# Up projections of a convolutional SwiGLU block, token-major, with their results turned by VectorE and GpSimd

## The chip, the cores and the metric

The kernel runs on one core of one Trainium2 chip. The metric is device time in microseconds (us); lower is better. A core has engines with a queue each: TensorE (PE; its weight loads are listed apart as PEld), VectorE (DVE), ScalarE (ACT), GpSimd (POOL) and SyncE (SP), which only starts DMAs. An engine takes the instructions of its queue in order, and waits at an instruction until what it needs has been signalled. Matmuls write to PSUM; everything else here lies in SBUF, 128 partitions wide, or in DRAM.

## The reference: what is computed

A trunk of two decoder layers on 256 tokens of width 2048, float32. Layer 0 mixes tokens by gated linear attention, layer 1 by attention over one shared key/value block; each is followed by the same channel mixer, which is what the change touches:

```python
def conv_ffn(x, norm_w, w_up, conv_w, conv_b, w_down):
    S = x.shape[1]
    h = rms_norm(x, norm_w) @ w_up                      # (256, 2048) @ (2048, 11264)
    hp = jnp.pad(h, ((0, 0), (CONV_WIDTH - 1, 0), (0, 0)))
    acc = conv_b
    for j in range(CONV_WIDTH):                         # 3 taps along the tokens
        acc = acc + conv_w[j] * hp[:, j:j + S]
    a, u = jnp.split(acc, 2, axis=-1)                   # 5632 gates, 5632 values
    return (jax.nn.silu(a) * u) @ w_down                # (256, 5632) @ (5632, 2048)
```

The norm factor of a token, 1/sqrt(mean of squares + eps), can be applied after the product, since it is one number per token.

## The kernel before

**Split products.** Every float32 operand is split into a high part of TensorE's rounded format and the rest. For weights ScalarE casts the high part (`whi`, line 143) and VectorE subtracts it (`wlo`, line 145), 1024 columns of a 128-partition tile at a time; such a 128x1024 piece is a *half*, and taking the next half is a *step* (`step`, line 343), the unit in which all delayed work is counted: `after(n, job)` runs a job n steps later. The input's parts lie side by side, 256 tokens high then 256 tokens low (`xw`). A product is high x high + low x high + high x low.

**Weight stream.** SP loads the weights in pieces of 1 MB (`wraw`, three buffers), in the order of `plan`, up to four pieces ahead; the splitting runs two halves ahead of TensorE, three where the plan says "deep" (`prefetch`, line 129), which it does for the up projections.

**The up projection** (`ffn`, line 693). A loop of 44 column groups per layer; group j holds 128 gate columns and the 128 value columns that belong to them. `gemm` (line 352) makes the group feature-major: the weights are the stationary operand (128x128), the input's tokens move past them, so that the result has features on partitions and tokens along the row. For each half, 8 products move 512 columns (both input parts against the weight's high part, line 359) and 8 move 256 (the input's high part against the weight's low part, line 361). ScalarE copies one part of the result out of PSUM (line 387), VectorE adds the other (line 388) and multiplies by the token norm (line 703). The convolution runs along the row, with one constant per partition for each tap: ScalarE makes the last tap with the bias (line 707), VectorE adds the two others (lines 709 and 711). ScalarE applies silu (line 713), VectorE multiplies gate and value (line 714), and the result is split into the `hid` tile (lines 399 and 400), one tile for two groups.

**The other form.** `gemm_tok` (line 365) makes 512 columns at a time token-major: the input is stationary, 512 weight columns move, and the result has tokens on partitions. Each half takes 12 products of 512 columns. Values, queries, keys and shared values use it; their results need tokens on partitions or are turned by TensorE.

**Beside the up projections.** The down projection (`down`, line 725) uses a scheme that saves products in blocks of four for some hidden tiles (marked in `ORDERS`). It needs sums of weights, which `make_ahead` (line 323) prepares while earlier stages run: every nine steps SP loads 1 MB of down weights into one of two `ahead` buffers, VectorE makes four sums (lines 328 and 329), and GpSimd's queue starts the store to DRAM (line 338). It also needs sums of hidden tiles (`comb`): some are made at once (`EARLY`), some are made at once and stored by GpSimd's queue (`ASIDE`, lines 676 to 685), some are made during the down projection at the place that `MADE` gives.

**Order.** The program is written with the tile framework, whose scheduler orders the instructions of each engine by its own timeline; `issue_after` ties an instruction behind another, mostly behind the latest weight split.

The norm of a stage is an object (`Norm`, line 402): `rows=True` gives the factor along a row on all partitions (through a product with ones, a logarithm and an exponential), `rows=False` as a column, one token per partition (through a power on GpSimd).

Of the kernel before, what the change touches and what calls it, by code (L numbers as in the profile page):

```python
# [42 lines left out]

EARLY = (1, 3)
ASIDE = (5, 7, 9, 11, 13, 15, 16)
MADE = {5: 0, 17: 1, 7: 1, 9: 2, 11: 3, 19: 4, 13: 5, 15: 6, 16: 7, 12: 9, 14: 11, 10: 8, 8: 10, 18: 6, 6: 4}
# [109 lines left out]
def trunk(ctx: ExitStack, tc: tile.TileContext, xT, cst, msk, w1p, w2a, w_k, w_qa, w_v2, w_v, w_g, w_go,  # L158
# [31 lines left out]
    plan = [(w_v2, 1, 16384), (w_v, 2, 8192), (w_k, 4, 4096), (w_qa, 4, 4096), (w_g, 8, 4096), (w_go, 8, 4096),  # L190
            (w_up0, FT, 4096), (w_dn0, 2, None),
            (w_mq, 4, 8192), (w_kk, 4, 8192), (w_kv, 4, 8192), (w_mo, 8, 4096),
            (w_up1, FT, 4096), (w_dn1, 2, None)]
# [126 lines left out]
    def after(steps, job):  # L320
        later.append((cur[0] + steps, job))

    def make_ahead(layer, w, first, every):

        def work(at):
            t = ws.buffer("+")
            b12, b11, b22, b21 = (t[:, 512 * i:512 * i + 512] for i in range(4))
            jobs = [lambda: V.tensor_sub(b22, b22, b12), lambda: V.tensor_sub(b12, b12, b11),  # L328
                    lambda: V.tensor_add(b11, b22, b11), lambda: V.tensor_sub(b21, b21, b11)]  # L329
            with tc.issue_after(ws.load.ins):  # L330
                nc.sync.dma_start(t, ws.rows(w, at[0], 2048 * at[1]))
# [6 lines left out]
            after(8, lambda: nc.gpsimd.dma_start(parked[layer][at], t))  # L338

        for i, at in enumerate(ahead[layer]):  # L340
            after(first + every * i, lambda at=at: work(at))

    def step(less=0):
        due = [job for at, job in later if at <= cur[0]]
# [289 lines left out]
        for n in norms:  # L634
            after(2, n.close)

    combos = {}
    rooms = []
    aside = dram.tile([2, len(ASIDE), 128, 768], F32R, name="aside")

# [21 lines left out]

    def combine(k, hid_k, halves_, kept=True):

        t = sums(halves_)
        own = room(k, hid_k, kept)
# [20 lines left out]
    def combine_parts(k, hid, kept):  # L687
# [2 lines left out]
            V.tensor_add(t, hid[k][:, :, :S], hid[k][:, :, S:])  # L690
        combine(k, hid[k], [(t[:, i, :128], t[:, i, 128:]) for i in range(2)], kept)

    def ffn(layer, nrm, then):
        xs = rows(nrm.xs)
        hid = []
        combos.clear()
        whole = [None, None]
        cw = C_CW + layer * 3 * 2 * FT
        cb = C_CB + layer * 2 * FT
        for j in range(FT):  # L700
            ps = gemm(xs, KT)
            t = both(ps, "up")
            V.tensor_mul(t, t, bc(nrm.rstd))  # L703
            au = temp("au")
            for i in range(2):
                n = i * FT + j
                A.activation(au[:, i, :], t[:, i, :], AF.Identity, bias=col(cb + n),  # L707
                             scale=col(cw + 2 * 2 * FT + n))
                V.scalar_tensor_tensor(au[:, i, 1:], t[:, i, :S - 1], col(cw + 2 * FT + n), au[:, i, 1:],  # L709
                                       op0=OP.mult, op1=OP.add)  # L710
                V.scalar_tensor_tensor(au[:, i, 2:], t[:, i, :S - 2], col(cw + n), au[:, i, 2:],
                                       op0=OP.mult, op1=OP.add)
            A.activation(au[:, 0, :], au[:, 0, :], AF.Silu)
            V.tensor_mul(au[:, 0, :], au[:, 0, :], au[:, 1, :])
            if j % 2 == 0:
                hid.append(slot([128, 2, 2 * S], F32R, "hid"))
            split(hid[-1][:, j % 2, :S], hid[-1][:, j % 2, S:], au[:, 0, :])
            whole[j % 2] = (au[:, 0, :128], au[:, 0, 128:])
            if j % 2 and j // 2 in EARLY:
                combine(j // 2, hid[-1], whole)  # L720
            if j % 2 and j // 2 in ASIDE:
                put_aside(layer, j // 2, hid[-1], whole)
        then(hid)

    def down(layer, hid, ready, jobs):
# [3 lines left out]
        for b, order in enumerate(ORDERS[layer]):  # L729
            new = [k for k, seven in order if seven and k not in done]  # L730
            done |= set(new)
            todo = dict(jobs.get(b, {}))
            for k in MADE:
                if k not in new:
                    continue
                kept = k in sevens[-1]
                todo.setdefault(MADE[k], []).append(
                    (lambda k=k: take_back(layer, k, hid[k])) if k in ASIDE else
                    (lambda k=k, kept=kept: combine_parts(k, hid, kept)))
# [24 lines left out]

            def comb(k, f):
                return combos[k][f]

            last = max(i for i, (k, seven) in enumerate(order) if seven)
            tail = [k for k, _ in order[len(order) - _tail(order):]]
            for i, (k, seven) in enumerate(order[:len(order) - len(tail)]):  # L770
                for job in todo.get(i, ()):
                    job()
                if seven:
                    prods((1, part(k, 0, 0), 0))
                    prods((3, comb(k, 3), 0), (2, part(k, 1, 0), 1))
# [130 lines left out]
            after(q - 3, lambda q=q: last_back(q))  # L906
        after(5, nrm.close)

    n_ffn = Norm(C_FN, "xw")
    project(rows(go), KT, [n_ffn])  # L910
    for p in range(NP):
        after(6 + 2 * p, lambda p=p: park(p))
# [151 lines left out]
        for c in range(2):  # L1064
            after(1 + c, lambda v=v, p=2 * g + c: values(v, p))

    n_ffn = Norm(C_FN + KT, "xw")
    project(rows(ox), KT, [n_ffn])

    for p in range(NP):  # L1070
# [37 lines left out]
    return _chunks(np.stack(rows_))  # L1108


def _pairs(w):
    k, n = w.shape
    j = n // 256
    return _chunks(w.reshape(k // 128, 128, 2, j, 128).transpose(3, 1, 0, 2, 4).reshape(j, 128, -1))


def _buckets():
# [63 lines left out]
```

## Time and profile before

| what | us |
|---|---|
| median of 3 runs | 2197.95 (2196.01 to 2198.8) |
| the profiled execution: its time | 2195.9 |
| its span, first to last instruction | 2194.1 |
| PE, DVE, ACT, POOL busy | 2186.3, 1794.4, 1322.8, 138.0 |
| first and last eviction of an up projection | 404.2, 1969.1 |

A row of the groups view gives the line of the kernel, engine, operation, the tiles written and read, shapes and count; after the first bar the busy time of the group and the mean ns of one instruction; after the second the idle time of the engine just ahead of them, and what ended it. A row of the timeline begins with start and duration in us. A row of the windows view gives a stretch of the span and how long each engine was busy in it.

### The profile page before, as it was taken

The numbers are of one execution on the slowest core, as the hardware profiler recorded it, in microseconds if no ns is written. First come the engines' busy times: TensorE is split into PE (matmuls) and PEld (weight loads), VectorE is DVE, ScalarE is ACT, GpSimd is POOL, SyncE is SP. The second block draws the span as 40 slices with busy tenths as digits, with TensorE's granted clock in tenths as the row PEclk, the third lists the DMA queues.
The fourth block names the chain that finished last, engine by engine and source line by source line (L and its number), as shares of the span: only waits on it lengthen the run. The fifth ranks groups of instructions, "written<-read, shape, count | busy, mean of one in ns | idle before, by whom it ended". The sixth has DMA issues, their size and how long they took to land.

```text
span 2194.1 us, 31287 instructions
## 1 busy us (share of the span) xinstructions
PE 2186.3 (100%) x11628; PEld 1887.8 (86%) x11628; DVE 1794.4 (82%) x2627; ACT 1322.8 (60%) x1862; POOL 138.0 (6%) x219
## 2 busy tenths in 40 slices
PE   9999999999999999999999999999999999999999
PEld 7889888888888888888888888888888888888887
DVE  7676877888889887877968787678988898878888
ACT  6655654666655555666656666446655565656575
POOL 0000000000000000000001343000000000000000
PEclk9999999999999999999999999999999999999999
DMA  7675778777787786887967788777788777868896
GB/s 290 213 283 181 264 263 318 272 269 279 282 293 276 277 293 211 310 329 263 357 248 290 274 299 289 246 271 274 275 295 299 281 283 284 286 223 310 322 352 252
DMA packets 113531, 613.14 MB, mean 279 GB/s; under 512 B 29361, under 2 KB 29889, under 8 KB 49634
## 3 DMA queue, kind: packets, MB, share of 16 engines
q1 hardware_dynamic: 94610, 523.75, 67.4%
q0 software_dynamic: 18048, 86.60, 10.4%
q8 instruction: 91, 1.49, 0.3%
q10 hardware_dynamic: 720, 0.79, 0.1%
q14 instruction: 62, 0.51, 0.1%
HBM read 535.31 MB, written 75.78 MB: 279 GB/s over the span
## 4 chain that ended last, share of the span: by engine, by line
PE 98%; DMA 1%; DVE 0%; ACT 0%; issue 0%; SPq 0%; ACTq 0%; DVEq 0%
PE acc L359 40%; PE acc L361 21%; PE acc L758 13%; PE acc L374 10%; PE p L758 5%; PE acc L377 5%; DMA wraw<-w_dn 1%; DMA wraw<-w_v 0%; PE sT L570 0%; DMA sums<-tsum 0%; PE tr L960 0%; PE s L978 0%; DVE wlo L145 0%; PE z L476 0%; PE o L456 0%; PE oT L456 0%
## 5 line engine op out<-in xcount | busy, mean ns | idle before, releaser
L143 ACT CAST whi<-wraw 128x1024 fp32r<-128x1024 f32 (+1 forms) x788 | 795.3, 1015 | 633.9 <-PE acc L359 306.4
L145 DVE TENSOR_TENSOR wlo<-wraw,whi 128x1024 fp32r<-128x1024 f32 (+1 forms) x788 | 916.5, 1176 | 266.7 <-ACT whi L143 89.8
L359 PE MATMUL acc<-xw,whi 128*128 128x512 f32 x3328 | 796.2, 391 | 0.0
L359 PEld LDWEIGHTS acc<-xw,whi 128*128 128x128 f32 x3328 | 611.2, 188 | 117.7
L361 PEld LDWEIGHTS acc<-xw,wlo 128*128 128x128 f32 x3328 | 427.2, 191 | 16.2
L361 PE MATMUL acc<-xw,wlo 128*128 128x256 f32 x3328 | 433.0, 283 | 0.0
L758 PE MATMUL acc<-whi,hid 128*128 128x512 f32 x588 | 169.1, 390 | 1.2 <-ACT whi L143 1.2
L145 DVE TENSOR_TENSOR wlo<-ahead,whi 128x1024 fp32r<-128x1024 f32 x98 | 119.0, 1222 | 29.3 <-ACT whi L143 15.6
L143 ACT CAST whi<-ahead 128x1024 fp32r<-128x1024 f32 x98 | 101.8, 1053 | 53.0 <-PE p L758 28.2
L758 PEld LDWEIGHTS acc<-whi,hid 128*128 128x128 f32 x588 | 109.6, 188 | 24.5 <-ACT whi L143 2.2
L374 PE MATMUL acc<-whi,xkv 128*128 128x512 f32 x512 | 129.9, 391 | 0.0
L374 PE MATMUL acc<-whi,xw 128*128 128x512 f32 x512 | 128.5, 391 | 0.9 <-DVE xw L260 0.6
L758 PE MATMUL p<-whi,hid 128*128 128x512 f32 x356 | 114.0, 389 | 0.0
L374 PEld LDWEIGHTS acc<-whi,xw 128*128 128x128 f32 x512 | 95.3, 188 | 21.3 <-issue 1.0
L374 PEld LDWEIGHTS acc<-whi,xkv 128*128 128x128 f32 x512 | 95.1, 188 | 18.9
L758 PE MATMUL acc<-whi,comb 128*128 128x512 f32 x348 | 102.2, 390 | 0.5 <-ACT whi L143 0.5
L707 ACT ACTIVATE au<-up,cs 128x256 f32<-128x256 f32 x176 | 96.1, 593 | 9.1 <-DVE up L703 8.8
L338 POOL DMA_DIRECT2D tsum<-ahead x58 | 31.5, 543 | 1096.2 <-DVE ahead L329 900.0
L709 DVE SCALAR_TENSOR_TENSOR au<-up,cs,au 128x255 f32<-128x255 f32 x176 | 82.7, 478 | 18.0 <-ACT au L707 17.9
L758 PE MATMUL acc<-wlo,hid 128*128 128x512 f32 x294 | 96.2, 389 | 0.0
L328 DVE TENSOR_TENSOR ahead<-ahead 128x512 f32<-128x512 f32 x116 | 79.4, 684 | 1.6 <-DMA ahead<-w_dn 1.4
L387 ACT COPY up<-acc 128x512 f32<-128x512 f32 x88 | 51.6, 586 | 47.0 <-PE acc L361 46.2
(266 smaller groups left out, 2309.0 us busy)
## 6 DMA issues: line engine op xcount, KB each, us to landing
wraw<-w_up SPq DMA_DIRECT2D x176, 1024.0 KB, 5.6
ahead<-w_dn SPq DMA_DIRECT2D x58, 1024.0 KB, 8.9
tsum<-ahead POOLq DMA_DIRECT2D x58, 1024.0 KB, 8.2
ahead<-tsum SPq DMA_DIRECT2D x49, 1024.0 KB, 6.2
wraw<-w_dn SPq DMA_DIRECT2D x58, 768.0 KB, 6.1
wraw<-w_dn SPq DMA_DIRECT2D x30, 1024.0 KB, 5.2
wraw<-w_g SPq DMA_DIRECT2D x16, 1024.0 KB, 4.9
wraw<-w_go SPq DMA_DIRECT2D x16, 1024.0 KB, 6.4
```

Of the source, the lines that this page charges most:

```text
L143: self.high = nc.scalar.copy(hi[:, a:b], src[:, a:b])
L145: self.low = nc.vector.tensor_sub(lo[:, a:b], src[:, a:b], hi[:, a:b].bitcast(F32))
L328: jobs = [lambda: V.tensor_sub(b22, b22, b12), lambda: V.tensor_sub(b12, b12, b11), lambda: V.tensor_add(b11, b22, b11), lambda: V.tensor_ ...
L338: after(8, lambda: nc.gpsimd.dma_start(parked[layer][at], t))
L359: T.matmul(ps[:, b, :], two[i][0][:, c:c + 128], xs(kt), start=kt == 0, stop=False)
L361: T.matmul(ps[:, b, :S], two[i][1][:, c:c + 128], xs(kt)[:, :S], start=False, stop=kt == kts - 1)
L374: T.matmul(ps[:, t, :], xs(kt)[:, x0 + 128 * t:x0 + 128 * t + 128], hi[:, c:c + 512], start=kt == 0 and x0 == 0, stop=False)
L377: T.matmul(ps[:, t, :], xs(kt)[:, 128 * t:128 * t + 128], lo[:, c:c + 512], start=False, stop=kt == KT - 1)
L387: A.copy(t, ps[:, :, S:])
L707: A.activation(au[:, i, :], t[:, i, :], AF.Identity, bias=col(cb + n), scale=col(cw + 2 * 2 * FT + n))
L709: V.scalar_tensor_tensor(au[:, i, 1:], t[:, i, :S - 1], col(cw + 2 * FT + n), au[:, i, 1:], op0=OP.mult, op1=OP.add)
L758: T.matmul(p[n], x[xi], w[wi][:, 512 * f:512 * f + 512], start=n not in begun, stop=left[n] == 0)
```

## The change

The up projections go through `gemm_tok`: 22 groups of 512 columns per layer in place of 44 of 256, the columns rearranged on the host so that a group holds gate, value, gate, value, 128 each. The result has tokens on partitions, and ScalarE applies the norm factor (a column now) as it copies each of the two token blocks out of PSUM. The convolution still wants features on partitions. So VectorE transposes each 128x512 block in squares of 32x32, which leaves every square turned but in the wrong place, and GpSimd copies the squares to their place: 16 copies per group, each from 32 partitions to 32 partitions with 256 elements in a row. Convolution and gate are cut into jobs that run 8 and 11 steps after the eviction (`UP_LAG`), the split and early sums one step further on. Two entries of `MADE` get a lag of four steps, with their slot taken at the old place. The up weights are no longer "deep".

```diff
+UP_LAG = (8, 11)
-MADE = {5: 0, 17: 1, 7: 1, 9: 2, 11: 3, 19: 4, ...
+MADE = {5: 0, 17: (1, 4), 7: 1, 9: 2, 11: 3, 19: (4, 4), ...
...
-            (w_up0, FT, 4096), (w_dn0, 2, None),
+            (w_up0, FT // 2, 8192), (w_dn0, 2, None),
...
-                ws.add(w, g, cols, w in (w_k, w_qa, w_g, w_go, w_up0, w_mo, w_up1))
+                ws.add(w, g, cols, w in (w_k, w_qa, w_g, w_go, w_mo))
...
+    def square(y, x):
+        for m in range(4):
+            xs_ = x[32 * m:32 * m + 32].rearrange("a t (n c b) -> a n t c b", c=4, b=32)
+            for c in range(4):
+                nc.gpsimd.tensor_copy(y[32 * c:32 * c + 32, :, :, 32 * m:32 * m + 32], xs_[:, :, :, c])
...
-        for j in range(FT):
-            ps = gemm(xs, KT)
-            t = both(ps, "up")
-            V.tensor_mul(t, t, bc(nrm.rstd))
+        def turn_up(g, ps):
+            x = slot([128, 2, 512], F32, "uT")
+            us = [temp("up", (128, 512)) for _ in range(2)]
+            for t in range(2):
+                with after_high():
+                    A.activation(us[t], ps[:, t, :], AF.Copy, scale=nrm.col[:, t:t + 1])
+                with after_low():
+                    V.transpose(x[:, t], us[t])
+            y = slot([128, 2, 2, S], F32, "up")
+            square(y.rearrange("p j i (t s) -> p (j i) t s", t=2), x)
+            for jj in range(2):
+                after(UP_LAG[jj], lambda jj=jj: conv(g, jj, y[:, jj]))
+        def conv(g, jj, t):
+            j = 2 * g + jj
+            au = temp("au")
...
+            after(1, lambda: gate(g, jj, au))
+        def gate(g, jj, au):
...
+            if jj and (g in EARLY or g in ASIDE):
+                two = [whole[0], whole[1]]
+                after(1, lambda: combine(g, hid[g], two) if g in EARLY else put_aside(layer, g, hid[g], two))
+        for g in range(FT // 2):
+            ps = gemm_tok(xs)
+            after(0, lambda g=g, ps=ps: turn_up(g, ps))
...
-    n_ffn = Norm(C_FN, "xw")
+    n_ffn = Norm(C_FN, "xw", rows=False)
...
-        "w_up0": _pairs(a["ffn_w_up"][0]),
+        "w_up0": _groups(_interleaved(a["ffn_w_up"][0]), 512),
```

More of the change, by code (lines that the diff above doesn't have):

```diff
@@ L41, in _order @@
     return [(int(k.rstrip("+^")), k[len(k.rstrip("+^")):]) for k in text.split()]
+UP_LAG = (8, 11)
 EARLY = (1, 3)
 ASIDE = (5, 7, 9, 11, 13, 15, 16)
-MADE = {5: 0, 17: 1, 7: 1, 9: 2, 11: 3, 19: 4, 13: 5, 15: 6, 16: 7, 12: 9, 14: 11, 10: 8, 8: 10, 18: 6, 6: 4}
+MADE = {5: 0, 17: (1, 4), 7: 1, 9: 2, 11: 3, 19: (4, 4), 13: 5, 15: 6, 16: 7, 12: 9, 14: 11, 10: 8, 8: 10, 18: 6, 6: 4}
 FIRST = "0 1+ 2 3+ 4 5+ 7+ 6 9+ 11+ 8 13+ 15+ 10 16+ 17+ 18 19+ 12+ 14+ 20 21"
@@ L190, in trunk @@
     plan = [(w_v2, 1, 16384), (w_v, 2, 8192), (w_k, 4, 4096), (w_qa, 4, 4096), (w_g, 8, 4096), (w_go, 8, 4096),
-            (w_up0, FT, 4096), (w_dn0, 2, None),
+            (w_up0, FT // 2, 8192), (w_dn0, 2, None),
             (w_mq, 4, 8192), (w_kk, 4, 8192), (w_kv, 4, 8192), (w_mo, 8, 4096),
-            (w_up1, FT, 4096), (w_dn1, 2, None)]
+            (w_up1, FT // 2, 8192), (w_dn1, 2, None)]
     for w, groups, cols in plan:
@@ L341, in make_ahead, with after_high, after_low @@
             after(first + every * i, lambda at=at: work(at))
+    def after_high():
+        return tc.issue_after(ws.high.ins)
+    def after_low():
+        return tc.issue_after(ws.low.ins)
     def step(less=0):
@@ L635, in project @@
             after(2, n.close)
-    combos = {}
+    combos, rooms_of = {}, {}
     rooms = []
@@ L663, in combine @@
     def combine(k, hid_k, halves_, kept=True):
+        own = room(k, hid_k, kept) if k not in combos else rooms_of[k]
         t = sums(halves_)
-        own = room(k, hid_k, kept)
         if own is not None and not kept:
@@ L696, in ffn @@
         combos.clear()
-        whole = [None, None]
         cw = C_CW + layer * 3 * 2 * FT
         cb = C_CB + layer * 2 * FT
-        for j in range(FT):
-            ps = gemm(xs, KT)
-            t = both(ps, "up")
-            V.tensor_mul(t, t, bc(nrm.rstd))
+        def turn_up(g, ps):
[12 more added lines that the diff above has]
+            j = 2 * g + jj
             au = temp("au")
@@ L706, in ffn @@
                 n = i * FT + j
[L707 to L710, printed above, removed]
+                with after_high():
+                    A.activation(au[:, i, :], t[:, i, :], AF.Identity, bias=col(cb + n),
+                                 scale=col(cw + 2 * 2 * FT + n))
+            for i in range(2):
+                n = i * FT + j
+                with after_low():
+                    V.scalar_tensor_tensor(au[:, i, 1:], t[:, i, :S - 1], col(cw + 2 * FT + n), au[:, i, 1:],
+                                           op0=OP.mult, op1=OP.add)
                 V.scalar_tensor_tensor(au[:, i, 2:], t[:, i, :S - 2], col(cw + n), au[:, i, 2:],
                                        op0=OP.mult, op1=OP.add)
-            A.activation(au[:, 0, :], au[:, 0, :], AF.Silu)
-            V.tensor_mul(au[:, 0, :], au[:, 0, :], au[:, 1, :])
-            if j % 2 == 0:
-                hid.append(slot([128, 2, 2 * S], F32R, "hid"))
[L717 to L722, printed above, removed]
+            after(1, lambda: gate(g, jj, au))
+        def gate(g, jj, au):
+            with after_high():
+                A.activation(au[:, 0, :], au[:, 0, :], AF.Silu)
+            with after_low():
+                V.tensor_mul(au[:, 0, :], au[:, 0, :], au[:, 1, :])
+            if jj == 0:
+                hid.append(slot([128, 2, 2 * S], F32R, "hid"))
+            split(hid[g][:, jj, :S], hid[g][:, jj, S:], au[:, 0, :])
+            whole[jj] = (au[:, 0, :128], au[:, 0, 128:])
+            if jj and (g in EARLY or g in ASIDE):
+                two = [whole[0], whole[1]]
+                after(1, lambda: combine(g, hid[g], two) if g in EARLY else put_aside(layer, g, hid[g], two))
+        whole = {}
+        for g in range(FT // 2):
+            ps = gemm_tok(xs)
+            after(0, lambda g=g, ps=ps: turn_up(g, ps))
         then(hid)
@@ L736, in down @@
                 kept = k in sevens[-1]
-                todo.setdefault(MADE[k], []).append(
+                at, lag = MADE[k] if isinstance(MADE[k], tuple) else (MADE[k], 0)
+                if lag:
+                    todo.setdefault(at, []).append(
+                        lambda k=k, kept=kept: rooms_of.update({k: room(k, hid[k], kept)}))
+                todo.setdefault(at + lag, []).append(
                     (lambda k=k: take_back(layer, k, hid[k])) if k in ASIDE else
@@ L1065, in trunk @@
             after(1 + c, lambda v=v, p=2 * g + c: values(v, p))
-    n_ffn = Norm(C_FN + KT, "xw")
+    n_ffn = Norm(C_FN + KT, "xw", rows=False)
     project(rows(ox), KT, [n_ffn])
@@ L1108, in _quads, with _interleaved @@
     return _chunks(np.stack(rows_))
-def _pairs(w):
+def _interleaved(w):
     k, n = w.shape
-    j = n // 256
-    return _chunks(w.reshape(k // 128, 128, 2, j, 128).transpose(3, 1, 0, 2, 4).reshape(j, 128, -1))
+    return w.reshape(k, 2, n // 256, 128).transpose(0, 2, 1, 3).reshape(k, n)
 def _buckets():
@@ L1166 @@
         "w_mo": _groups(a["moba_w_out"][0], 256),
-        "w_up1": _pairs(a["ffn_w_up"][1]),
+        "w_up1": _groups(_interleaved(a["ffn_w_up"][1]), 512),
         "w_dn1": _quads(a["ffn_w_down"][1], ORDERS[1]),
```

## The prediction

> **What bounds the kernel now.** I read the page first: busy shares, then the chain that ended last.
>
> ```profile
> span 2194.1 us, 31287 instructions
> PE 2186.3 (100%) x11628; PEld 1887.8 (86%) x11628; DVE 1794.4 (82%) x2627; ACT 1322.8 (60%) x1862; POOL 138.0 (6%) x219
> PE 98%; DMA 1%; DVE 0%; ACT 0%; issue 0%; SPq 0%; ACTq 0%; DVEq 0%
> ```
>
> The chain is TensorE almost alone (98%), so time is won where TensorE does the same work at a better pace and lost where another engine stops feeding it. GpSimd is nearly free (6%), VectorE is not (82%). A share over the whole span hides stages, so next come the two stretches of the up projections. The first starts one column group (11.14 us) ahead of the first eviction at 404.2 us and takes 44 groups, the second ends with the last eviction at 1969.1 us. These are the rows of the evictions, and the windows view of both stretches (columns: time with count for PE, weight loads, DVE, ACT, POOL; then granted clock, DMA share, GB/s):
>
> ```profile
> L387 ACT COPY up<-acc x88: 565/587/588, 404.2 to 1969.1; 128x512 f32<-128x512 f32 x88
> ```
>
> ```profile
> 393.00:883.00 490.00, 490.00 (x2812) 432.81 (x2811) 420.75 (x655) 295.72 (x420) 16.50 (x31) 1.00 0.77 274
> 1479.00:1969.00 490.00, 490.00 (x2819) 433.11 (x2819) 424.32 (x662) 294.67 (x419) 16.03 (x31) 1.00 0.79 275
> ```
>
> TensorE never pauses there, the clock is granted in full, and VectorE works 420.75 and 424.32 of 490 us: 86%. That is the figure to watch, because this change gives VectorE's neighbour GpSimd its first steady work.
>
> **TensorE's part.** The timeline shows the pace of both loop forms. In the up projection two weight halves (a block of 8 input tiles) repeat from one L359 row to the next; in the token-major query projection one half repeats from one L374 row to the next:
>
> ```profile
> 703.32 3.82 PE L359 MATMUL acc<-xw,whi 128*128 128x512 f32 x16
> 706.98 2.08 PE L361 MATMUL acc<-xw,wlo 128*128 128x256 f32 x16
> 708.89 3.82 PE L359 MATMUL acc<-xw,whi 128*128 128x512 f32 x16
> ```
>
> ```profile
> 1172.46 1.98 PE L374 MATMUL acc<-whi,xw 128*128 128x512 f32 x8
> 1175.18 1.98 PE L374 MATMUL acc<-whi,xw 128*128 128x512 f32 x8
> ```
>
> Before: 708.89 - 703.32 = 5.57 us for two halves. The 16 wide ones take 3.66 us (229 ns each), the 16 of 256 columns 1.91 us (119 ns each), a little more than half a wide one. After: the same columns in 12 products of 512 columns per half, 1175.18 - 1172.46 = 2.72 us. A pair of column groups has 8 halves: 4 x 5.57 = 22.28 us before, 8 x 2.72 = 21.76 us after. There are 22 pairs in each of two layers, so TensorE alone gains 44 x 0.52 = 22.9 us. This is the whole gain that I can find: bytes, chunks and the split of weights stay the same in number.
>
> **VectorE's part.** Its rows by shape, with two lines of ScalarE used below:
>
> ```profile
> L145 DVE TENSOR_TENSOR wlo<-wraw,whi 128x1024 fp32r<-128x1024 f32 x722 | 874.1, 1220 | 254.9 <-ACT whi L143 80.8 <-PE acc L361 76.3 <-issue 75.2
> L709 DVE SCALAR_TENSOR_TENSOR au<-up,cs,au 128x255 f32<-128x255 f32 x176 | 82.7, 478 | 18.0 <-ACT au L707 17.9
> L703 DVE TENSOR_TENSOR up<-up,rstd_h 128x512 f32<-128x512 f32 x88 | 60.4, 686 | 1.0
> L388 DVE TENSOR_TENSOR up<-up,acc 128x512 f32<-128x512 f32 x88 | 59.8, 679 | 0.1
> L387 ACT COPY up<-acc 128x512 f32<-128x512 f32 x88 | 51.6, 586 | 47.0 <-PE acc L361 46.2
> L823 DVE STREAM_TRANSPOSE hT<-h 128x512 f32<-128x512 f32 x8 | 5.6, 703 | 0.0
> L945 ACT ACTIVATE q<-acc,col_h 128x512 f32<-128x512 f32 x8 | 5.6, 696 | 0.0
> ```
>
> VectorE has (420.75 + 424.32) / 44 = 19.2 us of work in a pair. Out go two adds (L388) and two products with the norm (L703): 2 x (0.679 + 0.686) = 2.73 us. In come two transposes of 128x512, which the turn of h already does at 0.703: 1.41 us. Left are 17.9 us for a TensorE period of 21.76. Convolution, gate, splits and early sums only move later. By itself VectorE stays hidden, with 3.9 us to spare.
>
> **ScalarE's part.** Two copies at 0.586 out, two scaled evictions at about 0.696 (the query's, same shape, also out of PSUM) in: +0.2 us on 295.72 / 22 = 13.4 us per pair. Nothing, while its queue isn't held. It now holds one new wait: the first convolution instruction of a pair waits for GpSimd, and behind it in the queue stand casts of the next weight halves, for which VectorE's subtraction and then TensorE wait. If GpSimd is late, this is the way by which it stops TensorE.
>
> **GpSimd's part, the term that decides.** Each pair adds 16 copies of 32 partitions x 256 elements, 704 in all (the built program has 44 batches of 16). No such copy runs in the kernel before. The nearest rows are its memsets, in the timeline of GpSimd:
>
> ```profile
> 4.62 0.33 POOL L462 MEMSET zst<- 81x256 f32 x1
> 4.88 0.54 POOL L464 MEMSET smask<- 128x512 f32 x1
> 5.34 0.33 POOL L467 MEMSET zaug<- 17x256 f32 x1
> 5.60 0.13 POOL L465 MEMSET smask<- 128x8 f32 x1
> ```
>
> 256 elements take 0.33 us on 81 partitions and on 17, so few partitions save nothing. One follows the other after 0.26 us (4.62 to 4.88). A memset only writes; a copy reads each element as well. I bound the copy by 0.26 us (reading wholly hidden behind writing) and 0.54 us (the 512-element memset: as many elements written as the copy reads and writes together), and take 0.40, half way, as neither row has a read. So GpSimd is busy 16 x 0.40 = 6.4 us in a period of 21.76, which by itself is hidden too.
>
> But do the copies run beside VectorE? The trace has one GpSimd operation that reads SBUF, a power of 128x8. Three of its eight runs, each with VectorE's row at that time:
>
> ```profile
> 1127.47 1.27 DVE L145 TENSOR_TENSOR wlo<-wraw,whi 128x1024 fp32r<-128x1024 f32 x1
> 1127.47 1.64 POOL L950 TENSOR_TENSOR rr<-ss,mhalf 128x8 f32<-128x8 f32 x1 [3.42 <-DVE ss L948]
> ...
> 1218.67 1.23 DVE L145 TENSOR_TENSOR wlo<-wraw,whi 128x1024 fp32r<-128x1024 f32 x1
> 1218.73 2.68 POOL L950 TENSOR_TENSOR rr<-ss,mhalf 128x8 f32<-128x8 f32 x1 [2.60 <-DVE ss L948]
> ...
> 1245.88 1.23 DVE L145 TENSOR_TENSOR wlo<-wraw,whi 128x1024 fp32r<-128x1024 f32 x1 [0.56 <-ACT whi L143]
> 1245.89 2.74 POOL L950 TENSOR_TENSOR rr<-ss,mhalf 128x8 f32<-128x8 f32 x1
> ```
>
> Started just behind a subtraction with two SBUF inputs, the power takes 2.68 and 2.74 us, not 1.64: 1.04 and 1.10 us more, about what the subtraction still has to run (1.17 us at 1218.73). Started in the same instant it takes 1.64, and the subtraction 1.27 for its usual 1.22. So GpSimd's read waits for the running VectorE instruction, and the two take turns. With 8 elements read, the trace can't show how long VectorE waits in return; I take the whole copy, since it reads to its end. The Trainium skill (SBUF — State Buffer, "Who interferes with whom") has this as a rule: a VectorE instruction with two SBUF inputs contends with a GpSimd instruction that reads SBUF. By that rule the sum is the serial one below, without it TensorE's 21.76 us stands; the late powers agree with the rule for GpSimd's wait, and no row here shows VectorE's.
>
> Almost all of the 17.9 us are such instructions: subtractions, convolution, gate, splits, sums. Only the transposes (1.41 us) read one input. So a pair needs 17.9 + 16 x 0.40 = 24.3 us on a resource that only one of the two holds, against 21.76 on TensorE and 22.28 now. Copies under the transposes take off up to 1.4; VectorE's own in-order waits for ScalarE, which never let it be busy for all of a stretch, add about that; I let these cancel. Sum: 44 x (24.3 - 22.28) = +89 us.
>
> Break-even with the kernel before is a hold of (22.28 - 17.9) / 16 = 0.27 us a copy; the ends give 22.1 us (-8 us in all) and 26.5 us (+186 us). The Trainium skill (GPSIMD Engine Reference, "Elementwise — side-by-side cycle accounting") gives 512 elements of a tight loop 769 ns; half of that, 0.38 us, is an estimate from that page and would make +75 us.
>
> **Small terms.** The norm ahead of each up projection is now reduced by column, which drops two products and the logarithm and exponential and adds a GpSimd power (1.64 us); its result is first needed 8 halves later: zero. Weight splits run 2 halves ahead instead of 3: zero, since the query projection runs so at 2.72 us; uncovered, it makes VectorE's delays reach TensorE one step sooner. The last pairs' convolutions slide into the down projections, where hidden tiles 20 and 21 come last: zero; uncovered, one pair's chain, some 10 us a layer. On GpSimd's queue the stores of the weight sums stand behind the copies, and SP's next load into that buffer, with weight loads queued behind it, waits for the store:
>
> ```profile
> L338 POOL DMA_DIRECT2D tsum<-ahead x58: 531/533/600, 101.8 to 1888.3; - x58
> tsum<-ahead POOLq DMA_DIRECT2D x58, 1024.0 KB, 8.2
> ```
>
> A buffer comes round after 18 steps (49 us); load, four sums and store (8 steps, then 8.2 us) leave some 19 us, more than a batch of copies, so zero. In the built order some transposes wait for the slot of a set-aside tile, whose store stands on GpSimd's queue a batch earlier, and the loads that take the set-aside sums back for the down projection stand among the last two batches: zero at 6.4 us a batch, and part of rival 2 if a batch takes a period.
>
> **Sum.** The profiled execution took 2195.9 us (span 2194.1 and 1.8 around it); 2195.9 + 89 = 2285. The median 2197.95 lies 2 us above it, so 2287 for a median.
>
> **Rivals.** (1) *The copies cost VectorE nothing*, because it keeps its turn or the hold is under 0.24 us ((21.76 - 17.9) / 16). For it: the subtraction beside the power lost only 0.05 us, and 3.9 us per pair are idle. Against it: GpSimd waited a full microsecond, twice. Then TensorE's gain comes through: 2197.95 - 22.9 = 2175. This is the one on the other side. (2) *GpSimd becomes the bound by waiting*: each copy first waits for one subtraction (1.22 us, the row above) and then copies. With 0.53 us for about one DMA issue a pair this makes 16 x (1.22 + 0.40) + 0.53 = 26.5 us, +186 us, 2384. For it: 2.68 and 2.74 us. Against it: copies stand back to back and shorter instructions (0.478) lie between. (3) *SP is held by late stores*: some 32 sums fall into the up stretches; at 3 us each past the slack, +96 us, 2294; the 19 us speak against it. That the change doesn't take place is no rival: the built order has the wide products and the copies.
>
> **How the numbers follow.** Serial turns 0.47 (2190 to 2384); copies free 0.31 (2172 to 2182); GpSimd bound by waiting 0.14 (2350 to 2450); SP held 0.03; a tie close to break-even 0.05. A measurement here tells about 0.2%, 4 us. Faster: rival 1 and a little of the tie, 0.32; same 0.04; slower 0.64. The range takes in rival 1 and the upper end of the serial case: 2168 to 2400; the forecast's own range is 2190 to 2384.
>
> **What would show it.** Right: L374-type products at 2.72 us a half but with gaps on TensorE that VectorE ends; subtractions well over 1.22 us, or GpSimd copies of a microsecond, while the other works; a stretch of some 535 us in place of 490. Wrong: copies near 0.3 us beside subtractions of 1.22 and a stretch of 479 us. A copy held for under 0.27 us, or a VectorE that isn't held, turns the sign.

## The result, and the profile after

The changed kernel takes 2176.12 us (median of 4 runs, 2175.2 to 2176.7); the kernel before took 2197.12 us beside it (2196.01 to 2198.8). The ratio is 0.9903, 95% interval 0.9886 to 0.9921. I had forecast 2287 us. What came is rival 1, copies that cost no time, for which I had worked out 2175.

The page of the changed kernel: span, busy shares, the chain that ended last by engine, and the group of the new copies; behind it the source view of the copies' line (shortest, median and longest in ns).

```profile
span 2173.4 us, 29230 instructions
PE 2165.5 (100%) x10224; PEld 1815.1 (84%) x10224; DVE 1829.8 (84%) x2531; ACT 1311.9 (60%) x1849; POOL 659.4 (30%) x925
PE 98%; DMA 2%; DVE 0%; ACT 0%; issue 0%; ACTq 0%; DVEq 0%; SPq 0%
L705 POOL COPY up<-uT 32x256 f32<-32x256 f32 x704 | 520.9, 740 | 310.5 <-DVE uT L722 240.7
```

```profile
L705 POOL COPY up<-uT x704: 392/496/1478, 411.6 to 1965.7; 32x256 f32<-32x256 f32 x176
```

TensorE is still the whole chain. GpSimd has gone from 6% to 30%, yet no line of the chain is its own. A copy takes 740 ns on average, nearly twice my 0.40 us, though the shortest takes 392. So GpSimd waited as I feared, and TensorE didn't notice. The windows of both up stretches (columns as before):

```profile
393.00:872.00 479.00, 479.00 (x2117) 396.79 (x2116) 429.77 (x588) 285.84 (x404) 261.24 (x365) 1.00 0.75 276
1457.00:1936.00 479.00, 479.00 (x2135) 397.53 (x2134) 435.71 (x598) 284.36 (x402) 254.72 (x352) 1.00 0.78 282
```

The windows are 479 us wide by choice: 22 x 21.76, the length that I gave for the case in which I am wrong. That a stretch has this length, its own ends show: the products of the up projections run from 385.82 to 865.08 and from 1468.83 to 1948.09 us (rows in the part on why the prediction was wrong), 479.26 us each. The first window starts 7 us late and the second 12 us early, which changes little: VectorE's time between the true ends is 430.23 and 434.61. TensorE has no gap in any of them. VectorE works 429.77 and 435.71 of 479 us (90%): it is fuller than before, but not full.

Now the shapes that answer to those of before: the subtraction was 1220 ns, the convolution's first step 478.

```profile
L146 DVE TENSOR_TENSOR wlo<-wraw,whi 128x1024 fp32r<-128x1024 f32 x722 | 911.1, 1269 | 253.8 <-ACT whi L144 170.6 <-issue 43.2 <-PE acc L368 22.8
L740 DVE SCALAR_TENSOR_TENSOR au<-up,cs,au 128x255 f32<-128x255 f32 x176 | 89.2, 543 | 0.2
L722 DVE STREAM_TRANSPOSE uT<-up 128x512 f32<-128x512 f32 x88 | 58.3, 693 | 0.0
L720 ACT ACTIVATE up<-acc,col_h 128x512 f32<-128x512 f32 x88 | 55.2, 677 | 0.0
```

Instructions with two SBUF inputs have grown by some 50 to 65 ns on average, not by a copy's length each. The transposes, with one input, take 693 ns, no more than the 703 of my estimate. How the turns are taken, the timeline of one batch shows, first VectorE, then GpSimd:

```profile
605.20 1.22 DVE L146 TENSOR_TENSOR wlo<-wraw,whi 128x1024 fp32r<-128x1024 f32 x1
606.34 0.69 DVE L329 TENSOR_TENSOR ahead<-ahead 128x512 f32<-128x512 f32 x1
...
608.46 1.42 DVE L146 TENSOR_TENSOR wlo<-wraw,whi 128x1024 fp32r<-128x1024 f32 x1
609.81 0.88 DVE L330 TENSOR_TENSOR ahead<-ahead 128x512 f32<-128x512 f32 x1
```

```profile
608.37 13.83 POOL L705 COPY up<-uT 32x256 f32<-32x256 f32 x16 [6.92 <-DVE uT L722]
```

Ahead of the batch a subtraction takes 1.22 us and a sum 0.69; beside it 1.42 and 0.88. So a VectorE instruction that meets a copy loses 0.19 to 0.20 us. In those 13.83 us GpSimd makes 16 copies while VectorE makes some 16 instructions: about one copy for each instruction, each waiting for the one that runs. The records of all 704 copies say the same: 650 start while a VectorE instruction with two SBUF inputs runs, and each of them ends 0.25 to 0.31 us after that instruction, however long it still had to run; 50 start beside an idle VectorE and 4 beside a transpose, and these take some 0.40 us. This is the same turn-taking that I read from the powers of the trace before, but unequal: GpSimd waits for a whole VectorE instruction, VectorE for a part of a copy.

### The profile page after: what moved, and what is told of

Its sections match the earlier page's. It is cut to its first block, busy times and chain, and to the rows that moved or that the text cites. A ratio compares the mean times of both kernels' runs of the same rounds, so it can differ in the third digit from the quotient of the medians.

```text
span 2173.4 us, 29230 instructions
## 1 busy us (share of the span) xinstructions
PE 2165.5 (100%) x10224; PEld 1815.1 (84%) x10224; DVE 1829.8 (84%) x2531; ACT 1311.9 (60%) x1849; POOL 659.4 (30%) x925
## 4 chain that ended last, share of the span: by engine, by line
PE 98%; DMA 2%; DVE 0%; ACT 0%; issue 0%; ACTq 0%; DVEq 0%; SPq 0%
PE acc L381 40%; PE acc L384 20%; PE acc L803 13%; PE acc L366 11%; PE acc L368 6%; PE p L803 5%; DMA wraw<-w_dn 1%; PE sT L577 0%; DMA sums<-tsum 0%; DMA ahead<-tsum 0%; PE tr L1005 0%; PE s L1023 0%; DVE wlo L146 0%; DMA h<-xT 0%; PE z L483 0%; PE o L463 0%
## 5 line engine op out<-in xcount | busy, mean ns | idle before, releaser
L146 DVE TENSOR_TENSOR wlo<-wraw,whi 128x1024 fp32r<-128x1024 f32 (+1 forms) x788 | 954.3, 1221 | 266.6 <-ACT whi L144 179.8
L381 PE MATMUL acc<-whi,xw 128*128 128x512 f32 x3328 | 825.5, 389 | 0.6 <-DVE xw L261 0.6
L381 PEld LDWEIGHTS acc<-whi,xw 128*128 128x128 f32 x3328 | 623.5, 188 | 130.4 <-issue 1.1
L705 POOL COPY up<-uT 32x256 f32<-32x256 f32 x704 | 520.9, 740 | 310.5 <-DVE uT L722 240.7
L384 PE MATMUL acc<-wlo,xw 128*128 128x512 f32 x1664 | 445.9, 389 | 0.0
L384 PEld LDWEIGHTS acc<-wlo,xw 128*128 128x128 f32 x1664 | 312.1, 188 | 65.0 <-DVE wlo L146 0.3
L366 PE MATMUL acc<-xw,whi 128*128 128x512 f32 x512 | 124.5, 392 | 0.0
L366 PEld LDWEIGHTS acc<-xw,whi 128*128 128x128 f32 x512 | 93.6, 188 | 17.7
L742 DVE SCALAR_TENSOR_TENSOR au<-up,cs,au 128x254 f32<-128x254 f32 x176 | 90.2, 543 | 0.0
L740 DVE SCALAR_TENSOR_TENSOR au<-up,cs,au 128x255 f32<-128x255 f32 x176 | 89.2, 543 | 0.2
```

Source lines behind the costliest of these rows:

```text
L146: self.low = nc.vector.tensor_sub(lo[:, a:b], src[:, a:b], hi[:, a:b].bitcast(F32))
L366: T.matmul(ps[:, b, :], two[i][0][:, c:c + 128], xs(kt), start=kt == 0, stop=False)
L381: T.matmul(ps[:, t, :], xs(kt)[:, x0 + 128 * t:x0 + 128 * t + 128], hi[:, c:c + 512], start=kt == 0 and x0 == 0, stop=False)
L384: T.matmul(ps[:, t, :], xs(kt)[:, 128 * t:128 * t + 128], lo[:, c:c + 512], start=False, stop=kt == KT - 1)
L705: nc.gpsimd.tensor_copy(y[32 * c:32 * c + 32, :, :, 32 * m:32 * m + 32], xs_[:, :, :, c])
```

## The experiments

Two theories. *Short hold*: a copy stops VectorE only for a part of its time, in proportion to what it reads; the rest of the copy is hidden, and time is lost only where hold or waiting grows until VectorE or GpSimd fills the 21.76 us of a pair. *No contest*, the rival: the two engines don't hold each other, and the 0.2 us have another cause (writes, the memory's load, the new order). Beside both stands the reason of my forecast, the *whole hold*.

**1. No copies.** The convolution reads the transposed tile as it lies; the 704 copies go.

```diff
-            y = slot([128, 2, 2, S], F32, "up")
-            square(y.rearrange("p j i (t s) -> p (j i) t s", t=2), x)
+            y = x.rearrange("p a (i s) -> p a i s", i=2)
```

> Leaves out the 16 GpSimd copies per group, so the convolution reads squares in the wrong place and the result is not the reference's. Theory (a copy holds VectorE for 0.19 us only, and that is covered): VectorE's subtractions go back to 1.22 us, VectorE's work per pair to about 17.9 us, and the time stays at 2176 us, within 4. Rival (the copies do cost time on the path, say by gaps at the ends of the stretches or by late convolutions): 2165 us or less.

Measured: 2175.39 us (2174.52 to 2177.23), ratio 0.9899 [0.9884, 0.9914]. The page's busy shares, the two stretches, and the subtraction:

```profile
PE 2165.0 (100%) x10224; PEld 1814.9 (84%) x10224; DVE 1728.3 (80%) x2531; ACT 1310.8 (60%) x1849; POOL 139.4 (6%) x221
...
393.00:872.00 479.00, 479.00 (x2116) 396.65 (x2116) 381.10 (x588) 286.02 (x404) 16.80 (x31) 1.00 0.77 280
1457.00:1936.00 479.00, 479.00 (x2133) 397.33 (x2132) 389.65 (x601) 285.34 (x402) 14.65 (x27) 1.00 0.79 284
...
L146 DVE TENSOR_TENSOR wlo<-wraw,whi 128x1024 fp32r<-128x1024 f32 x722 | 876.5, 1220 | 352.9 <-ACT whi L144 268.8 <-issue 41.8 <-PE acc L368 22.5
```

By the medians the copies cost the kernel 0.7 us (2176.12 against 2175.39), which these intervals can't tell from nothing. They cost VectorE 1829.8 - 1728.3 = 101.5 us of busy time, 0.144 us a copy. Without them VectorE needs (381.10 + 389.65) / 44 = 17.5 us a pair; with them 17.5 + 16 x 0.144 = 19.8, still below 21.76.

**2. The same, with 16 memsets a pair into a tile that nobody reads.** It adds to the first edit

```diff
+            z = slot([128, 1024], F32, "z")
+            for m in range(4):
+                for c in range(4):
+                    nc.gpsimd.memset(z[32 * c:32 * c + 32, 256 * m:256 * m + 256], 0.0)
```

> As the run without copies, but GpSimd writes 16 blocks of 32 partitions x 256 elements per group with memsets into a tile that nobody reads (result not the reference's). Theory (only GpSimd's reads hold VectorE): subtractions stay at 1.22 us beside the memsets, time 2176 us. Rival (any GpSimd access to SBUF holds VectorE): subtractions of some 1.4 us beside them, as beside the copies.

Measured: 2176.73 us (two runs, 2176.65 and 2176.8), ratio 0.9904 [0.9884, 0.9924]. GpSimd's memsets, a batch of them, and a subtraction beside it:

```profile
L727 POOL MEMSET z<- 32x256 f32 x704 | 215.1, 305 | 101.4 <-ACT au L751 53.0 <-ACT whi L144 22.1
...
642.62 5.45 POOL L727 MEMSET z<- 32x256 f32 x16
...
642.63 1.23 DVE L146 TENSOR_TENSOR wlo<-wraw,whi 128x1024 fp32r<-128x1024 f32 x1 [0.88 <-ACT whi L144]
```

Sixteen writes in 5.45 us, 0.34 us each, hardly more than the 0.33 us of the trace before, and the subtraction keeps its 1.23 us. So it is the copies' reading that meets VectorE; "writes" as the cause is out.

**3. Copies of twice the length**, 512 elements from the transposed tile into two tiles that nobody reads; the convolution reads as in 1.

```diff
+            z, xf = [slot([128, 1024], F32, "z") for _ in range(2)], x.rearrange("p t n -> p (t n)")
+            for m in range(4):
+                for c in range(4):
+                    nc.gpsimd.tensor_copy(z[m // 2][32 * c:32 * c + 32, 512 * (m % 2):512 * (m % 2) + 512],
+                                          xf[32 * m:32 * m + 32, :512])
```

> As the run without copies, but GpSimd makes 16 copies of 32 partitions x 512 elements per group into tiles that nobody reads (result not the reference's): twice the elements, the same number of instructions. Theory (the hold is the time of the read, so in proportion to elements): a subtraction beside a copy takes about 1.60 us (1.22 + 2 x 0.19); if 0.11/0.19 of the copies hit one, VectorE needs 17.9 + 16 x 0.22 = 21.4 us of 21.76 and the time is 2176 us to 2200; if all hit, 24 us and 2275. Rival (a fixed price per instruction): 1.41 us and 2176 us.

Measured: 2405.94 us (2403.89 to 2408.44), ratio 1.095 [1.0932, 1.0969]. A subtraction beside a batch, and TensorE's longest wait (total, times, longest):

```profile
636.82 1.63 DVE L146 TENSOR_TENSOR wlo<-wraw,whi 128x1024 fp32r<-128x1024 f32 x1
```

```profile
PE acc L381 <- ACT up L720: 93.4, 16, 9.1
```

The hold has doubled with the length: 1.63 for 1.22. The time is far above both forecasts, and can't be put down to the hold alone: TensorE waits 93.4 us for evictions, a wait that the changed kernel doesn't have. I put that down to the two extra tiles, which also take slots, so that the order changes; that is not shown. It was a flaw of the edit, and experiment 5 mends a part of it.

**4. The real copies, each in two halves** of 128 elements: the same bytes, twice the instructions.

```diff
-                nc.gpsimd.tensor_copy(y[32 * c:32 * c + 32, :, :, 32 * m:32 * m + 32], xs_[:, :, :, c])
+                for n in (0, 2):
+                    nc.gpsimd.tensor_copy(y[32 * c:32 * c + 32, n:n + 2, :, 32 * m:32 * m + 32], xs_[:, n:n + 2, :, c])
```

> The changed kernel with each copy cut in two of 128 elements, 32 per group, with the right result. Theory (hold in proportion to elements): a VectorE instruction beside a copy is 0.10 us longer instead of 0.19, VectorE's work per pair stays at about 19.7 us, time 2176 us. Rival (a fixed price per copy): 0.19 us again, VectorE at 17.9 + 32 x 0.11 = 21.4 us per pair or more, time 2176 to 2230 us.

Measured: 2211.94 us (2211.66 to 2213.1), ratio 1.0065 [1.005, 1.008]: slower than the kernel before. The page's chain by engine, the copies, a subtraction beside them, one batch with what follows it, and ScalarE's longest wait (total, times, longest):

```profile
PE 59%; POOL 28%; DVE 7%; issue 2%; DMA 2%; ACT 1%; POOLq 0%; DVEq 0%; ACTq 0%; SPq 0%
...
L706 POOL COPY up<-uT 32x128 f32<-32x128 f32 x1408 | 812.1, 602 | 177.6 <-DVE uT L723 144.7 <-PE acc L384 3.0 <-PE acc L381 2.3
L706 POOL COPY up<-uT x1408: 284/388/1342, 411.4 to 2009.0; 32x128 f32<-32x128 f32 x176
...
643.57 1.31 DVE L146 TENSOR_TENSOR wlo<-wraw,whi 128x1024 fp32r<-128x1024 f32 x1
...
640.70 19.33 POOL L706 COPY up<-uT 32x128 f32<-32x128 f32 x32 [3.06 <-DVE uT L723]
660.46 0.98 DVE L741 SCALAR_TENSOR_TENSOR au<-up,cs,au 128x255 f32<-128x255 f32 x2 [2.55 <-ACT au L736]
662.14 1.29 DVE L723 STREAM_TRANSPOSE uT<-up 128x512 f32<-128x512 f32 x2
663.57 1.82 POOL L706 COPY up<-uT 32x128 f32<-32x128 f32 x2 [2.53 <-DVE uT L723]
...
ACT au L736 <- POOL up L706: 219.8, 42, 7.8
```

VectorE loses less (1788.6 us busy on the page against 1829.8; 0.09 us for an instruction that is met), as the theory says, and the kernel loses 36 us, which the theory (2176 us) did not say. Half a copy still takes 602 ns on average, 284 at the shortest: the rest is its wait for a VectorE instruction. A batch fills 19.33 of 21.76 us, and a loop closes: the batch, then the convolution that ScalarE begins, then the next group's transposes, which stand behind this convolution on VectorE, then the next batch. From one batch to the next that takes 663.57 - 640.70 = 22.87 us, and GpSimd has 28% of the chain. This is GpSimd bound by waiting, as in my rival 2. The path is only in part the one that I had named for it: the casts behind the convolution cost TensorE 14.4 us of waits in the up projections, and the transposes behind it I had not seen. The halves bring the loop about, the whole copies don't.

**5. Experiment 3 with one unread tile** for the layer, so that no slots are taken in the loop (`z = slot([128, 1024], F32, "z")` ahead of it, all copies into `z`).

> As the earlier 512-element run (16 copies of 32 x 512 per group that nobody reads, the convolution reads the turned tile in place, result not the reference's), but all copies write one tile that is taken once per layer, so that no slot changes hands and the order on ScalarE and VectorE stays that of the run without copies. Theory (the hold is the read: 0.41 us for 512 elements, about 69% of the copies hit a VectorE instruction, as 94.7 us over 704 copies at 0.195 say): VectorE 17.5 + 16 x 0.28 = 22.0 us per pair against TensorE's 21.76, time 2180 to 2200 us, 2290 if all hit. Rival (the serial sum of the prediction with the copy's whole duration of some 0.6 to 0.7 us): 17.5 + 16 x 0.65 = 27.9 us per pair, 2440 us.

Measured: 2320.28 us (2317.85 to 2322.86), ratio 1.0554 [1.0538, 1.057]. The copies; the windows of the up stretches, which end later here; a window at the start of the first down projections, with GpSimd's first rows in it; and in the last line the same window of the changed kernel from 872 us on:

```profile
L729 POOL COPY z<-uT 32x512 f32<-32x512 f32 x704 | 669.8, 951 | 72.0 <-DVE uT L724 23.0 <-PE acc L384 9.2
L729 POOL COPY z<-uT x704: 599/692/6091, 411.1 to 2158.4; 32x512 f32<-32x512 f32 x176
...
386.00:871.00 485.00, 480.55 (x2116) 397.62 (x2115) 431.11 (x569) 277.87 (x391) 247.77 (x268) 1.00 0.74 270
1528.00:2014.00 486.00, 481.22 (x2116) 398.05 (x2115) 437.83 (x578) 277.73 (x393) 250.37 (x267) 0.99 0.76 274
869.00:937.00 68.00, 54.14 (x180) 38.71 (x180) 68.00 (x79) 32.70 (x52) 61.65 (x66) 0.82 0.58 198
...
871.79 0.54 POOL L692 DMA_DIRECT2D comb<-aside  x1 [3.35 <-PE acc L384]
872.38 21.42 POOL L729 COPY z<-uT 32x512 f32<-32x512 f32 x22
```

```profile
872.00:940.00 68.00, 68.00 (x302) 56.32 (x301) 64.49 (x98) 48.73 (x70) 14.54 (x20) 1.00 0.88 328
```

Here my forecast's picture does appear: from 869 to 937 us VectorE has no gap, GpSimd copies for 61.65 of 68 us, and TensorE works 54.14. VectorE's cost is (1905.6, its busy time on this page, - 1728.3) / 704 = 0.252 us a copy, so a pair needs 17.5 + 16 x 0.252 = 21.5 of 21.76 us, which leaves next to nothing. The up stretches themselves lose little, 485 and 486 us for 479. Of the 144.7 us by which the span grows they have 13; some 52 fall between them and some 79 behind the second. There the order of this build has copies in GpSimd's queue behind and between the loads that take the set-aside sums back, as at 872 us, and TensorE waits 28.2 us for such loads. The time lies above both values of the theory (2180 to 2200, and 2290 if all hit) and below the whole hold's 2440; how the 144 us divide between hold and order stays open.

**6. The real copies twice**, the second time into an unread tile.

```diff
             square(y.rearrange("p j i (t s) -> p (j i) t s", t=2), x)
+            square(z.rearrange("p (n t s) -> p n t s", n=4, t=2), x)
```

> The changed kernel with a second set of 16 copies behind the first in each group, into a tile that nobody reads; the result stays right. Theory (GpSimd gets one copy per VectorE instruction, 0.74 us each on average, so it is its own queue that binds): 32 x 0.74 + 0.53 = 24.2 us per pair, time 2176 + 44 x 2.4 = 2283 us, with ScalarE waiting for GpSimd. Rival (VectorE binds): 17.5 + 32 x 0.135 = 21.8 us per pair, 2178 us.

Measured: 2356.01 us (2353.86 to 2360.58), ratio 1.0719 [1.0703, 1.0735]. GpSimd in one pair, the load in the chain of that window, VectorE's wait for it, and all such waits (total, times, longest):

```profile
641.57 9.84 POOL L705 COPY up<-uT 32x256 f32<-32x256 f32 x16 [1.46 <-DVE uT L724]
651.46 12.09 POOL L705 COPY z<-uT 32x256 f32<-32x256 f32 x16
663.50 0.54 POOL L339 DMA_DIRECT2D tsum<-ahead  x1
...
654.22 8.25 DMA ahead<-w_dn
...
662.56 0.73 DVE L329 TENSOR_TENSOR ahead<-ahead 128x512 f32<-128x512 f32 x1 [4.14 <-DMA ahead<-w_dn]
...
DVE ahead L329 <- DMA ahead<-w_dn: 41.1, 19, 4.4
```

9.84 + 12.09 + 0.54 = 22.5 us on GpSimd for a period of 21.76: it is over-full. The store of a weight sum stands behind the copies, the next load into a buffer of this kind comes late, and VectorE stands still in order behind the sum that needs it. In the chain from 640 to 690 us that load has 30.3%. This is what rivals 2 and 3 described, at twice the copies. The theory had GpSimd's fill right and the path wrong: ScalarE waits only 10.3 us for GpSimd in the whole run, and the time is 73 us above the 2283 that it gave. Over the whole run the chain has PE 79%, DVE 6%, DMA 5%, POOL 4%; how the 180 us divide among these stays open. VectorE's share of it is small: its busy time grew by 147.9 us on experiment 1 (1876.2 on this page), 0.105 us for each of 1408 copies.

**7. The kernel before, with 16 idle copies a pair** of 256 elements, out of its normed input into an unread tile.

```diff
+            if j % 2:
+                xf = nrm.xs[0][:, 0, :S].bitcast(F32)
+                for m in range(4):
+                    for c in range(4):
+                        with tc.issue_after(ws.low.ins):
+                            nc.gpsimd.tensor_copy(z[32 * c:32 * c + 32, 256 * m:256 * m + 256], xf[32 * m:32 * m + 32])
```

> The kernel before with 16 copies of 32 x 256 per two column groups on GpSimd, from the input tile into a tile that nobody reads; the result stays right. Theory (a copy holds a VectorE instruction for 0.195 us, 0.135 on average): VectorE goes from 19.2 to 21.4 us of 22.28 per pair, subtractions beside copies take 1.41 us, and the time stays at 2198 us, within 5. Rival (the prediction's price, 0.40 us a copy): 25.6 us per pair, 2340 us.

Measured: 2197.45 us (2196.63 to 2200.0), ratio 0.9999 [0.999, 1.0009]. Copies, and a subtraction beside one:

```profile
L710 POOL COPY z<-xw 32x256 f32<-32x256 f32 x704 | 535.3, 760 | 40.3
...
656.23 1.41 DVE L145 TENSOR_TENSOR wlo<-wraw,whi 128x1024 fp32r<-128x1024 f32 x1
```

The copies behave in the old order as in the new (760 ns, subtractions of 1.41), and cost nothing there either, with 19.2 us of VectorE work a pair beside them and 0.117 us more for each copy (1877.0 us busy on this page against 1794.4). So the new order isn't the cause of the 0.2 us, and neither are writes, by 2.

**8. The real copies on ScalarE**, in four jobs of four behind its casts (`nc.scalar.copy` in place of `nc.gpsimd.tensor_copy`, `after(3 + m, ...)`).

> The changed kernel with the 16 copies of a group on ScalarE in place of GpSimd, four in each of the steps 3 to 6 after the eviction; the result stays right. Theory (nobody shares VectorE's second read with ScalarE): subtractions 1.22 us, VectorE 17.5 us per pair; ScalarE 13.0 + 16 x 0.40 = 19.4 us of 21.76, time 2176 us, within 5, if the casts behind the copies are still in time. Rival (a ScalarE with 89% load makes the casts late): gaps on TensorE that end with a cast, 2190 to 2250 us.

Measured: 2180.46 us (2177.82 to 2181.2), ratio 0.9916 [0.9901, 0.993]. The copies there and the subtraction:

```profile
L706 ACT COPY up<-uT 32x256 f32<-32x256 f32 x704 | 284.3, 404 | 10.0 <-DVE uT L726 0.8
L146 DVE TENSOR_TENSOR wlo<-wraw,whi 128x1024 fp32r<-128x1024 f32 x722 | 875.4, 1222 | 296.2 <-ACT whi L144 212.3 <-issue 41.8 <-PE acc L368 22.4
```

ScalarE makes such a copy in 404 ns, and VectorE keeps its 1222 ns: this reader isn't in VectorE's way. The same bytes are read and written here, so the memory's load isn't the cause either, and *no contest* falls. The edit wins nothing (the intervals of the ratios, 0.9916 and 0.9903, overlap), since the changed kernel was bound by TensorE already. No version tried is faster than it beyond the measurement.

## Why the prediction was wrong

**TensorE's part was right.** The first product of the up projection and the first of the down projection in each layer, before and then after:

```profile
385.81 3.82 PE L359 MATMUL acc<-xw,whi 128*128 128x512 f32 x16
875.89 0.63 PE L758 MATMUL acc<-whi,hid 128*128 128x512 f32 x2
1478.81 3.36 PE L359 MATMUL acc<-xw,whi 128*128 128x512 f32 x14
1968.89 0.63 PE L758 MATMUL acc<-whi,hid 128*128 128x512 f32 x2
```

```profile
385.82 2.00 PE L381 MATMUL acc<-whi,xw 128*128 128x512 f32 x8
865.08 0.61 PE L803 MATMUL acc<-whi,hid 128*128 128x512 f32 x2
1468.83 2.00 PE L381 MATMUL acc<-whi,xw 128*128 128x512 f32 x8
1948.09 0.62 PE L803 MATMUL acc<-whi,hid 128*128 128x512 f32 x2
```

A stretch went from 490.08 to 479.26 us, 10.8 us a layer and 21.6 in both; 0.8 us of it is lost between the stretches, so that 20.8 show at the last of these rows. The sum had 22.9: my 5.57 us stood on two stamps, and each 0.01 in it is 1.8 us in 44 pairs.

**VectorE's and ScalarE's own work was right**: 17.5 us a pair in experiment 1 for my 17.9; ScalarE's scaled eviction took 677 ns for 696, and (285.84 + 284.36) / 44 = 13.0 us a pair for 13.6.

**The step that failed** is in GpSimd's part: "With 8 elements read, the trace can't show how long VectorE waits in return; I take the whole copy, since it reads to its end." Beside an idle VectorE a copy of the changed kernel took 0.392 to 0.405 us, so my 0.40 for a copy was right, with some luck, since it was the middle between two rows without a read; the hold that I set equal to it was not. VectorE loses 0.19 to 0.20 us where it meets a copy, and 0.144 us a copy on average: 50 of the 704 copies start beside an idle VectorE, and the rest of the difference stays open. The term of the sum was 16 x 0.40 = 6.4 us a pair and measured 16 x 0.144 = 2.3. My own sum with that gives 17.9 + 2.3 = 20.2 us, below TensorE's 21.76, and so rival 1's time. The condition of rival 1 (a hold under 0.24 us) and its 2175 held; its other condition, that VectorE keeps its turn, did not.

**What led me there.** The powers of the trace before showed only GpSimd's side: it waits for the VectorE instruction that runs. I took the other side to be equal. The row that spoke against it stood beside them, a subtraction that lost 0.05 us beside a power of 1.64; I discounted it for its 8 elements. The Trainium skill (SBUF — State Buffer, "SBUF: two separate sides") says of a VectorE instruction with two SBUF inputs and a GpSimd one that reads SBUF that whichever starts first gets the shared port pair for the whole instruction, and that the other fully blocks. For GpSimd behind VectorE the runs agree (650 copies of the changed kernel end 0.25 to 0.31 us after the instruction that ran when they started). For VectorE behind GpSimd they don't: the hold was 0.09, 0.19 and 0.41 us for copies of 128, 256 and 512 elements that take 0.284, 0.392 and 0.599 us at the shortest. At all three lengths that is the copy's own time less some 0.2 us, so of these the longest comes nearest to the rule. The Trainium skill (the same page, "Who interferes with whom") says that a GpSimd instruction that only writes doesn't contend, and that ScalarE never waits for anyone; experiments 2 and 8 agree (subtractions of 1220 ns beside the memsets; ScalarE's copies took 399 to 412 ns).

**The small terms.** ScalarE's wait for GpSimd, which I costed at nothing with casts behind it, is not among the longest waits of the changed kernel, and is 219.8 us with the halves: the cover is GpSimd's slack, 21.76 us less a batch (13.83 us in the row above). The stores behind copies were right at zero in the changed kernel; experiment 6 shows the price when a pair's copies fill the period. The norm by column, the shorter lead of the splits and the sliding last pairs show no wait on TensorE.

**Rivals 2 and 3** had the right mechanisms and the wrong point. I had each copy wait for a whole subtraction and then copy (1.62 us); a copy waits for what is left of whatever runs, often an instruction of 0.4 to 0.9 us, and took 0.740 on average. Not shown is at which number of copies between 16 and 32 the loss begins.

## What to carry to other kernels

When two engines take turns, measure both sides: how long A waits for B says nothing of how long B waits for A. Here the steady partner lost 0.19 us where the other waited up to a whole instruction, so the number of instructions on the waiting side counts: splitting the copies cost 36 us at the same bytes. Look at the length too: copies twice as long held VectorE for 0.41 us. Then ask of the sum for the bounding engine's period, 17.5 + 2.3 against 21.76, before calling a shared path a bottleneck.

## What was not expected of the hardware

- The hold of VectorE by a GpSimd read went with the elements read, some 0.7 to 0.8 ns each (0.09 us for 128, 0.19 for 256, 0.41 for 512), and GpSimd's wait with what the VectorE instruction still had to run. Halving a copy therefore halved the hold and saved only 740 - 602 = 138 ns of a copy's time.
- A copy can lose more than one turn: in experiments 5 and 7 the longest took 6.09 and 4.26 us, longer than any VectorE instruction there, while the longest of the changed kernel took 1.48. What decides this is not shown.
- A copy of 32 partitions x 256 elements took as long on ScalarE (404 ns) as the shortest on GpSimd (392 ns).
- Gaps on TensorE cost twice. In experiment 5 the granted clock was 0.82 in the window from 869 to 937 us, where TensorE paused for 14 of 68 us, and 1.00 and 0.99 in the up stretches, where it paused for less than 5 of 485; over the run it was 0.976. In that window a product took 54.14 / 180 = 0.30 us, and 68.00 / 302 = 0.23 us in the same window of the changed kernel. The Trainium skill (TensorE: Matmul & The Clock Gate, "Part 1: The HAM clock gate (the "warmup" mystery)") says that the clock is throttled by default and that activity releases it; these rows agree.
